# The scan's norms summed in four groups of 32 columns and spread by DMA, and output blocks fetched and split in pairs k, k+4

## The chip, the cores and the metric

The kernel runs on one NeuronCore of a Trainium2 chip. TensorE (PE) multiplies, VectorE (DVE) and ScalarE (ACT) do elementwise work, GpSimd (POOL) does a little, and SyncE (SP) issues nearly all DMAs, in order, from one queue. The metric is the device time of one execution in microseconds; lower is better.

## The reference

One layer of a hybrid encoder over 2048 tokens of width 1024: RMSNorm, an input projection, two mixers (a gated short convolution and a Mamba-2 scan), an output projection over both mixers' 2 x 1024 outputs, then a squared-ReLU MLP and a final RMSNorm. The part that the change touches is the grouped norm after the scan, and how its result enters the output projection:

```python
gated = (y * jax.nn.silu(z)).reshape(b, t, SSD_GROUPS, SSD_INNER // SSD_GROUPS)
gated = rmsnorm(gated, norm_w.reshape(SSD_GROUPS, SSD_INNER // SSD_GROUPS))
...
y = jnp.concatenate([y_a, y_b], axis=-1)
x = x + jnp.einsum("btc,cd->btd", y, w_out)
```

There are two groups of 512 channels. For every token and group one number is needed: the reciprocal root of the mean of 512 squares.

## The kernel before

Channels lie on partitions, tokens on the free axis. Tokens come in four blocks of 512 (TB); a block has four chunks of 128 (L). Every product in fp32 is made of three fp32r matmuls, high by high, low by high and high by low (`mm3`, L118 to L120, or L315 to L317 in `chain`), so every operand is split first: a cast on ACT gives the high part, a subtraction on DVE the low part. A tile framework decides the instruction order of each engine when the program is built; the order is then fixed.

The stages around the change, in order of time in the profile:

- `second_half` (about 440 to 950 us): the second half of the input projection, with scan chunks 0 to 15 (blocks 0 and 1) run beside it. At its end the scan's buffers are given back and the loads `rb<-ym_d` (L379) of the output projection's first operands take their place; the loads `wraw<-w_out` (L98) and `xt<-x` (L1643) follow in the same SP queue.
- `Output.pair` (to about 1040 us): the products of mixer A for blocks 0 and 1, a seven-product scheme.
- `Output.unit` 16 to 63 (to about 1350 us): units of 24 matmuls into a tile `pm`, first mixer A for blocks 2 and 3, then mixer B. Scan chunks 16 to 31 (blocks 2 and 3) run beside them. Units 48 to 63 take blocks 2 and 3 of mixer B; unit 50 is the first of block 3.

A norm is made at the last chunk of each block and group (`Scan.back`), eight times. `ssq` [128 x 512] holds the sums of squares over four channel tiles. It is split into `ahi` and `alo` (L180, L181), two matmuls with a matrix of ones sum over partitions and at the same time copy the sum to all 128 partitions (`pss`, L186, L187), then come root (L188, ACT) and reciprocal (L189, DVE), both on 128 x 512. For blocks 0 and 1 the result is stored (`rn_d<-ssq`, L1499) and loaded back as `rn` when it is needed (L1519); for blocks 2 and 3 it stays in SBUF.

`Output.fetch` loads two neighbouring channel tiles (`ry`, L1607), k and k+1. `Output.fill` scales each with its norm (mixer B, L1619), casts it (L1623) and subtracts (L1624), each [128 x 512], into `uh` and `ul`; a tile pair k and k+4 shares one `uh` buffer. Tiles 0 to 3 belong to group 0, tiles 4 to 7 to group 1. A unit multiplies k = 0 to 7 in that order.

Of the kernel before, what the change touches and what calls it, by code (L numbers as in the profile page):

```python
# [11 lines left out]
F32 = mybir.dt.float32  # L12
F32R = mybir.dt.float32r
AF = mybir.ActivationFunctionType
ALU = mybir.AluOpType

P = 128
# [23 lines left out]
def trunk(ctx: ExitStack, tc: tile.TileContext, x, w_in, w_dt, w_out, w_up, w_down, cvec, hrow, out):  # L41
# [19 lines left out]
    ym_d = [dram.tile([P, 7, TB], F32, name=f"ym_d{k}") for k in range(4)]  # L61
    wide = lambda n, k: [dram.tile([P, k, TH], F32, name=f"{n}_d{h}") for h in range(2)]
    xs_d, sz_d, ys_d, yn_d = wide("xs", 12), wide("sz", 8), wide("ys", 8), wide("yn", 8)
    rn_d = dram.tile([P, NBB, G, TB], F32, name="rn_d")
    dt_d = [dram.tile([P, 4, NC * 16], F32, name=f"dt_d{b}") for b in range(NB)]
    rd_d = [dram.tile([2, NC * 16, P], F32, name=f"rd_d{b}") for b in range(NB)]
    pd_d = dram.tile([P, TB], F32, name="pd_d")
# [20 lines left out]
    def col(base, i):  # L88
        return cv[:, base + i : base + i + 1]
# [1253 lines left out]
    class Scan:  # L1343
# [104 lines left out]
        def back(self, n):  # L1448

            b, g, c, h, ts, r0 = self.place(n)  # L1450
            t = self.got.pop(n)
            cT = t["bc"][:, 1]
            byhead = lambda a: a.rearrange("p (h d) -> p h d", h=HG)
            state = self.state[g]
            st = psum("tp", "st", 2)
            mm3(st, *t["btok"], *t["parts"], 0, 1)
            yo = psum("k4", "yo")
            for j in range(4):
                nc.tensor.matmul(yo[:, j * L : (j + 1) * L], state[:, j * P : (j + 1) * P], cT, start=True, stop=True)  # L1459
            yd = t["yd"]  # L1460
            for i in range(HG):
                nc.tensor.matmul(  # L1462
                    yd[(i % 2) * 64 : (i % 2) * 64 + 64, (i // 2) * L : (i // 2 + 1) * L],
                    byhead(t["xdt"])[:, i, :],
                    t["dec"][:, i % 2 * 4 + i // 2, :],
                    start=False,
                    stop=True,
                    skip_group_check=True,
                )
            y = t["y"]  # L1470
            t1 = self.tmp()
            nc.vector.tensor_tensor(out=byhead(state), in0=byhead(state), in1=t["cdec"], op=ALU.mult)
            nc.vector.tensor_tensor(out=state, in0=state, in1=st, op=ALU.add)
            nc.vector.tensor_tensor(out=t1, in0=yo, in1=t["eb"].rearrange("p j l -> p (j l)"), op=ALU.mult)
            nc.vector.tensor_tensor(out=t1, in0=t1, in1=yd, op=ALU.add)
            yield
            t3 = t1.rearrange("p (j l) -> p j l", j=4)
            nc.vector.tensor_tensor(out=y, in0=t3, in1=y, op=ALU.mult)
            yield
            nc.sync.dma_start(yn_d[h][:, 4 * g : 4 * g + 4, ts], y)  # L1480
            q4 = self.tmp().rearrange("p (j l) -> p j l", j=4)
            self.act = nc.scalar.activation(q4, y, AF.Square)
            nc.vector.tensor_tensor(out=q4[:, 0:2], in0=q4[:, 0:2], in1=q4[:, 2:4], op=ALU.add)
            if c == 0:
                self.ssq = self.sum_tile(b, g)
            ssq = self.ssq
            nc.vector.tensor_tensor(out=ssq[:, c * L : (c + 1) * L], in0=q4[:, 0], in1=q4[:, 1], op=ALU.add)
            if c == NC - 1:
                st = Rstd(None, self.part_tile, 512, TB)
                st.parts(ssq)  # L1490
            yield
            if c == NC - 1:
                if (b, g) == (NBB, 0):
                    ssq = uh.tile([P, TB], F32, tag="uh3", name="ssq", bufs=4)
                st.whole(ssq, "mw" if h else "tp")
                if h:
                    self.rn[b, g] = ssq
                else:
                    nc.sync.dma_start(rn_d[:, b, g], ssq)  # L1499
            yield  # L1500
            yield

# [4 lines left out]
                return self.tile([TB], "ssq", 1)  # L1507
            return uh.tile([P, TB], F32, tag="uh3", name="ssq", bufs=4)

        def part_tile(self, name):  # L1510
            if self.bufs == 1:
                return proj.e(name, TB)
            return uh.tile([P, TB], F32, tag="ul3", name=name, bufs=4)

        def norm(self, b, g):

            if (b, g) not in self.rn:
                t = self.rn[b, g] = uh.tile([P, TB], F32, tag="ul3", name="rn", bufs=4)
                nc.sync.dma_start(t, rn_d[:, b, g])  # L1519
            return self.rn[b, g]  # L1520

        def run(self, begin, end):
# [65 lines left out]
    class Output:  # L1588
# [14 lines left out]
        def fetch(self, i, b, k, raw):  # L1603

            t = raw("ry")
            src = (ys_d, yn_d)[i][b // NBB]
            nc.sync.dma_start(t, src[:, k : k + 2, b % NBB * TB : (b % NBB + 1) * TB])  # L1607
            return t

        def fill(self, i, b, c, k, t):  # L1610

            blk = self.y.setdefault((i, b), {})
            for n in range(2):
                f = k + n
                if f < 4:
                    self.places[f][c] = proj.place(c)
                hi, lo = (a[:, f // 4] for a in self.places[f % 4][c])
                if i:
                    nc.vector.scalar_tensor_tensor(  # L1619
                        out=t[:, n], in0=t[:, n], scalar=col(C_NSSD, f), in1=scan.norm(b, f // 4), op0=ALU.mult, op1=ALU.mult  # L1620
                    )
                with tc.issue_after(scan.act.ins) if (i, b) in ((1, 0), (1, 2)) else nullcontext():
                    nc.scalar.copy(hi, t[:, n])  # L1623
                nc.vector.tensor_tensor(out=lo, in0=t[:, n], in1=hi.bitcast(F32), op=ALU.subtract)  # L1624
                blk[f] = (hi, lo)

        def open(self, stack, ws):
            self.xp = stack.enter_context(tc.tile_pool(name="xp", bufs=1, reuse_waits="tile"))
# [69 lines left out]
        def unit(self, n, hook):  # L1698

            i, b, d = self.UNITS[n]  # L1700
            self.residual(n + 1)
            m = (2 * i + b // 2) * KD + d
            if b % 2 == 0:
                self.weights(m + 2)
            pm = psum("mm", "pm")
            whi, wlo = self.ws[m]
            for k in range(KD):
                if k == KD // 2:
                    hook(2 * n)
                mm3(pm, whi[:, k, :], wlo[:, k, :], *self.y[i, b][k], k, KD)  # L1710
            t = self.xt.pop(n)
            nc.vector.tensor_tensor(out=t, in0=pm, in1=t, op=ALU.add)
            nc.sync.dma_start(x1_d[b][:, d], t)
            if i and b < NBB:
                self.square(b, d, t)
            hook(2 * n + 1)
# [11 lines left out]
        def schedule(self):  # L1728
# [3 lines left out]

            def put(i, b, c, load, splits):
                def fetch():
                    held[i, b] = [self.fetch(i, b, k, self.raw) for k in range(0, KD, 2)]
                    if i and b < NBB:
                        for g in range(G):
                            scan.norm(b, g)

                self.todo.setdefault(load, []).append(fetch)  # L1740
                for j, at in enumerate(splits):
                    self.todo.setdefault(at, []).append(lambda j=j: self.fill(i, b, c, 2 * j, held[i, b][j]))

            put(0, 3, 0, 20, (22, 23, 23, 24))
            put(0, 2, 2, 25, (26, 27, 32, 32))
# [141 lines left out]
```

## Time and profile before

| what | us |
|---|---|
| median of 3 runs | 2596.71 (2595.24 to 2597.68) |
| profiled execution | 2599.74 |
| its span | 2598.0 |
| PE busy, of the span | 2572.3 |
| DVE busy | 1937.1 |
| ACT busy | 1407.0 |

The profiled execution is 1.74 us longer than its span and 3.03 us above the median of the runs. In a timeline, a row shows the start in us, the duration in us, engine, line, operation, output and input tiles, shapes, and in brackets how long the engine was idle before it and what ended the idle time. Matmuls overlap, so the distance of two starts is what a matmul costs, not its duration. In a view by stretches each engine's busy time in the stretch is given, then the granted PE clock, the busy share of the DMA engines and GB/s.

### The profile page before, as it was taken

To read this page: it belongs to the slowest core of one execution; us is meant where nothing else is said; L and a number is where in the kernel's file an instruction comes from. 1 tells how busy PE (TensorE), PEld (TensorE's weight loads), DVE (VectorE), ACT (ScalarE), POOL (GpSimd) and SP (SyncE) were. 2 spreads that over 40 slices of the span, in tenths; PEclk is the share of its full clock that TensorE was granted. 3 is DMA by queue.
4 is the path that set the end of the run, shared out by engine and by line. 5 is a ranking of instruction groups with operands and counts; after the bars stand their busy time and mean duration, and the time that the engine had idled before them with its cause. 6 is when DMAs were issued, how large, how long until landed. Compare 5 with 4: busy or idle time off the path is not lost.

```text
span 2598.0 us, 33641 instructions
## 1 busy us (share of the span) xinstructions
PE 2572.3 (99%) x12027; PEld 2120.2 (82%) x12027; DVE 1937.1 (75%) x2627; ACT 1407.0 (54%) x2147; POOL 79.2 (3%) x99
## 2 busy tenths in 40 slices
PE   9999999999999999999999999999999999999998
PEld 7788878788888878888888888888887888888887
DVE  8877777867778688889877765644448887888885
ACT  6554345876567566656336555755556444444433
POOL 2110010000000000000000000000000000000001
PEclk9999999999999999999999999999999999999999
DMA  4555665755555478997656885855557655665762
GB/s 175 175 191 188 218 238 184 238 171 174 178 168 176 158 251 281 291 294 243 201 186 231 300 313 219 291 196 212 183 201 252 187 175 154 219 207 179 238 203 78
DMA packets 256345, 546.40 MB, mean 210 GB/s; under 512 B 26673, under 2 KB 93873, under 8 KB 256177
## 3 DMA queue, kind: packets, MB, share of 16 engines
q1 hardware_dynamic: 255600, 543.34, 62.4%
q8 instruction: 94, 1.54, 0.2%
q10 hardware_dynamic: 576, 0.92, 0.1%
q14 instruction: 75, 0.61, 0.1%
HBM read 359.87 MB, written 184.29 MB: 209 GB/s over the span
## 4 chain that ended last, share of the span: by engine, by line
PE 88%; DVE 5%; DMA 3%; issue 2%; ACT 2%; POOL 0%; SPq 0%; POOLq 0%; DVEq 0%; ACTq 0%
PE px L315 14%; PE px L317 14%; PE px L316 14%; PE py L315 7%; PE py L316 7%; PE py L317 7%; PE pm L118 4%; PE pm L119 4%; PE pm L120 4%; PE pw L315 3%; PE pw L317 3%; PE pw L316 3%; PE yd L1462 1%; DVE ul L391 1%; PE yo L1459 1%
## 5 line engine op out<-in xcount | busy, mean ns | idle before, releaser
L315 PE MATMUL px<-uh,whi 128*128 128x512 f32 x1736 | 679.6, 392 | 7.7 <-DVE acc L1176 3.3
L317 PE MATMUL px<-uh,wlo 128*128 128x512 f32 x1736 | 676.2, 390 | 0.5 <-DVE wlo L104 0.5
L316 PE MATMUL px<-ul,whi 128*128 128x512 f32 x1736 | 675.8, 389 | 0.0
L315 PEld LDWEIGHTS px<-uh,whi 128*128 128x128 f32 x1736 | 325.9, 188 | 82.2 <-DVE acc L1176 4.1
L317 PEld LDWEIGHTS px<-uh,wlo 128*128 128x128 f32 x1736 | 325.9, 188 | 70.9 <-issue 1.8
L316 PEld LDWEIGHTS px<-ul,whi 128*128 128x128 f32 x1736 | 326.0, 188 | 66.3
L104 DVE TENSOR_TENSOR wlo<-wraw,whi 128x512 fp32r<-128x512 f32 (+1 forms) x213 | 219.0, 1029 | 197.4 <-ACT whi L103 196.4
L103 ACT CAST whi<-s 128x1024 fp32r<-128x1024 f32 x218 | 228.3, 1047 | 216.6 <-PE py L316 97.7
L315 PE MATMUL py<-uh,whi 128*128 128x512 f32 x868 | 339.2, 391 | 2.3 <-ACT eb L850 1.5
L103 ACT CAST whi<-wraw 128x1024 fp32r<-128x1024 f32 x214 | 192.2, 899 | 274.5 <-PE px L316 214.1
L317 PE MATMUL py<-uh,wlo 128*128 128x512 f32 x868 | 338.0, 389 | 0.0
L316 PE MATMUL py<-ul,whi 128*128 128x512 f32 x868 | 338.0, 389 | 0.0
L104 DVE TENSOR_TENSOR wlo<-s,whi 128x1024 fp32r<-128x1024 f32 x218 | 265.1, 1216 | 76.2 <-ACT whi L103 75.2
L118 PE MATMUL pm<-uh,whi 128*128 128x512 f32 (+1 forms) x520 | 200.1, 385 | 0.8 <-ACT z L601 0.7
L119 PE MATMUL pm<-ul,whi 128*128 128x512 f32 (+1 forms) x520 | 197.8, 381 | 0.5 <-DVE ul L231 0.5
L120 PE MATMUL pm<-uh,wlo 128*128 128x512 f32 (+1 forms) x520 | 197.5, 380 | 0.0
L315 PEld LDWEIGHTS py<-uh,whi 128*128 128x128 f32 x868 | 163.0, 188 | 38.6 <-ACT eb L850 1.9
L316 PEld LDWEIGHTS py<-ul,whi 128*128 128x128 f32 x868 | 163.0, 188 | 34.2 <-issue 0.8
L317 PEld LDWEIGHTS py<-uh,wlo 128*128 128x128 f32 x868 | 163.0, 188 | 33.8
L315 PE MATMUL pw<-uh,whi 128*128 128x512 f32 x434 | 169.3, 390 | 0.0
L316 PE MATMUL pw<-ul,whi 128*128 128x512 f32 x434 | 168.9, 389 | 0.0
L317 PE MATMUL pw<-uh,wlo 128*128 128x512 f32 x434 | 168.9, 389 | 0.0
(265 smaller groups left out, 3613.1 us busy)
## 6 DMA issues: line engine op xcount, KB each, us to landing
hid_d<-e SPq DMA_DIRECT2D x96, 512.0 KB, 3.6
rh<-hid_d SPq DMA_DIRECT2D x96, 512.0 KB, 4.3
wraw<-w_in SPq DMA_DIRECT2D x68, 512.0 KB, 4.0
wraw<-w_down SPq DMA_DIRECT2D x104, 256.0 KB, 3.6
wraw<-w_up SPq DMA_DIRECT2D x48, 512.0 KB, 4.6
dec<-rd_d SPq DMA_DIRECT2D x32, 512.0 KB, 5.4
wraw<-w_out SPq DMA_DIRECT2D x32, 512.0 KB, 5.6
sums_d<-s SPq DMA_DIRECT2D x32, 512.0 KB, 4.4
```

What stands on the lines that cost most here:

```text
L103: nc.scalar.copy(hi, raw)
L104: split["last"] = eng.tensor_tensor(out=lo, in0=raw, in1=hi.bitcast(F32), op=ALU.subtract)
L118: nc.tensor.matmul(out, whi, hi, start=(k == 0), stop=False)
L119: nc.tensor.matmul(out, whi, lo, start=False, stop=False)
L120: nc.tensor.matmul(out, wlo, hi, start=False, stop=(k == nk - 1))
L315: nc.tensor.matmul(p, hi, h[0], start=not seeded and k == 0, stop=False, **kw)
L316: nc.tensor.matmul(p, hi, h[1], start=False, stop=False, **kw)
L317: nc.tensor.matmul(p, lo, h[0], start=False, stop=(k == len(g) - 1), **kw)
L391: nc.vector.tensor_tensor(out=p[i][1], in0=t, in1=p[i][0].bitcast(F32), op=ALU.subtract)
L1459: nc.tensor.matmul(yo[:, j * L : (j + 1) * L], state[:, j * P : (j + 1) * P], cT, start=True, stop=True)
L1462: nc.tensor.matmul(yd[(i % 2) * 64 : (i % 2) * 64 + 64, (i // 2) * L : (i // 2 + 1) * L], byhead(t["xdt"])[:, i, :], t["dec"][:, i % 2 * 4 ...
```

## The change

The sums over partitions are made by four fp32 matmuls (`pn`), each with 32 columns of ones as weights and one chunk's 128 columns of `ssq` as moving data, into 32 partitions each of one PSUM tile. So `ssq` isn't split. Root and reciprocal work on 128 x 128. The result (128 x 128, of which rows 0, 32, 64 and 96 hold the four chunks) is stored for every norm; a second DMA reads these four rows and spreads them over 128 partitions as [128 x 512]. For blocks 0 and 1 this load stands where `rn` was loaded before; for blocks 2 and 3 it follows the store.

`fetch` loads tiles k and k+4 in one piece. `fill` scales both with their two norms, and makes one cast and one subtraction of [128 x 1024]. A unit multiplies in the order 0, 4, 1, 5, 2, 6, 3, 7.

```diff
@@ Scan.back
             nc.vector.tensor_tensor(out=ssq[:, c * L : (c + 1) * L], in0=q4[:, 0], in1=q4[:, 1], op=ALU.add)
+            yield
             if c == NC - 1:
-                st = Rstd(None, self.part_tile, 512, TB)
-                st.parts(ssq)
-            yield
-            if c == NC - 1:
-                if (b, g) == (NBB, 0):
-                    ssq = uh.tile([P, TB], F32, tag="uh3", name="ssq", bufs=4)
-                st.whole(ssq, "mw" if h else "tp")
+                pn = psum("mw", "pn") if h else psum("tp", "pn", 2)
+                for i in range(NC):
+                    nc.tensor.matmul(
+                        pn[i * 32 : i * 32 + 32, 0:L], ones[:, 0:32], ssq[:, i * L : (i + 1) * L], start=True, stop=True
+                    )
+                r = ssq[:, 0:L]
+                nc.scalar.activation(r, pn[:, 0:L], AF.Sqrt, bias=eps, scale=1.0 / 512)
+                nc.vector.reciprocal(out=r, in_=r)
+                nc.sync.dma_start(rn_d[b][g], r)
                 if h:
-                    self.rn[b, g] = ssq
-                else:
-                    nc.sync.dma_start(rn_d[:, b, g], ssq)
+                    self.rn[b, g] = self.norm_tile(b, g, "uh3" if (b, g) == (NBB, 0) else None)
@@ Scan
+        def norm_tile(self, b, g, tag):
+            t = uh.tile([P, TB], F32, tag=tag, name="rn", bufs=4) if tag else self.ssq
+            row = rn_d[b][g].rearrange("(q p) l -> p q l", p=32)[0]
+            nc.sync.dma_start(t.rearrange("p (q l) -> p q l", q=NC), row.partition_broadcast(P))
+            return t
@@ Output.fetch
-            nc.sync.dma_start(t, src[:, k : k + 2, b % NBB * TB : (b % NBB + 1) * TB])
+            nc.sync.dma_start(t, src[:, k : k + 5 : 4, b % NBB * TB : (b % NBB + 1) * TB])
@@ Output.fill
+            hi, lo = self.places[k][c] = proj.place(c)
+            if i:
+                for n in range(2):
+                    nc.vector.scalar_tensor_tensor(
+                        out=t[:, n], in0=t[:, n], scalar=col(C_NSSD, k + 4 * n), in1=scan.norm(b, n), op0=ALU.mult, op1=ALU.mult
+                    )
+            with tc.issue_after(scan.act.ins) if (i, b) in ((1, 0), (1, 2)) else nullcontext():
+                nc.scalar.copy(hi, t)
+            nc.vector.tensor_tensor(out=lo, in0=t, in1=hi.bitcast(F32), op=ALU.subtract)
             for n in range(2):
...
+                blk[k + 4 * n] = hi[:, n], lo[:, n]
@@ Output.unit
-            for k in range(KD):
+            for j in range(KD):
...
+                k = j // 2 + j % 2 * 4
+                mm3(pm, whi[:, k, :], wlo[:, k, :], *self.y[i, b][k], j, KD)
```

The built order of the instructions moves with it. Three places, each as it stands before and with the change.

The first is the end of `second_half`: the last norm of block 1 on DVE, from its sum of squares (L1487) on. `wlo` are weight splits, `s` weight sums, `eb` and `ea` evictions of the projection. Before:

```order
L1487 TENSOR_TENSOR ssq<-stmp 128x128
L181 TENSOR_TENSOR alo<-ssq,ahi 128x512
L269 TENSOR_TENSOR s_7941<-wraw 128x512
L234 TENSOR_TENSOR s_7941<-s_7941,wraw 128x512
L807 TENSOR_TENSOR eb<-px,s_7908 128x512
L234 TENSOR_TENSOR s_7985<-wraw 128x512
L189 RECIPROCAL ssq<-ssq 128x512
L104 TENSOR_TENSOR wlo<-s_7941,whi 128x1024
```

With the change:

```order
L1487 TENSOR_TENSOR ssq<-stmp 128x128
L104 TENSOR_TENSOR wlo<-wraw,whi 128x1024
L269 TENSOR_TENSOR s_7940<-wraw 128x512
L1497 RECIPROCAL ssq<-ssq 128x128
L234 TENSOR_TENSOR s_7940<-s_7940,wraw 128x512
L807 TENSOR_TENSOR eb<-px,s_7907 128x512
L234 TENSOR_TENSOR s_7984<-wraw 128x512
L104 TENSOR_TENSOR wlo<-s_7940,whi 128x1024
```

The split of `ssq` is gone, and the reciprocal stands before two weight sums and one eviction that it stood behind. On SP the store of this norm stays right behind `yn_d<-y`, with the loads `rb<-ym_d` behind it.

The second is DVE at the last norm, that of block 3 and group 1, and the operands of unit 50 (`ry` into `ul`). `xt<-pm` are evictions of units. Before, from the reciprocal on:

```order
L189 RECIPROCAL ssq<-ssq 128x512
L1712 TENSOR_TENSOR xt<-pm,xt 128x512
L104 TENSOR_TENSOR wlo<-wraw,whi 128x1024
L1726 TENSOR_TENSOR facc<-sq,facc 128x512
L1619 SCALAR_TENSOR_TENSOR ry<-ry,cv,ssq 128x512
L1712 TENSOR_TENSOR xt<-pm,xt 128x512
L1619 SCALAR_TENSOR_TENSOR ry<-ry,cv,ssq 128x512
L1624 TENSOR_TENSOR ul_11350<-ry,uh_11349 128x512
L181 TENSOR_TENSOR alo<-facc,ahi 128x512
L1624 TENSOR_TENSOR ul_11355<-ry,uh_11354 128x512
```

With the change, from the first scale that needs this norm:

```order
L1618 SCALAR_TENSOR_TENSOR ry<-ry,cv,ssq 128x512
L1713 TENSOR_TENSOR xt<-pm,xt 128x512
L1618 SCALAR_TENSOR_TENSOR ry<-ry,cv,ssq 128x512
L1623 TENSOR_TENSOR ul_11309<-ry,uh_11308 128x1024
L1618 SCALAR_TENSOR_TENSOR ry<-ry,cv,ssq 128x512
L1623 TENSOR_TENSOR ul_11329<-ry,uh_11328 128x1024
L189 RECIPROCAL facc<-facc 128x512
L1623 TENSOR_TENSOR ul_11361<-ry,uh_11360 128x1024
L1713 TENSOR_TENSOR xt<-pm,xt 128x512
L1618 SCALAR_TENSOR_TENSOR ry<-ry,cv,ssq 128x512
L189 RECIPROCAL facc<-facc 128x512
L1623 TENSOR_TENSOR ul_11385<-ry,uh_11384 128x1024
```

Before, four halves of group 0 were split further up, and only the four of group 1 waited for this norm; now all four pieces do, and two reciprocals of the next stage (`facc`) stand between them.

The third is PE at the same norm: a `pm` matmul of unit 47 is ahead of it and behind it in both. Before:

```order
L118 MATMUL pm<-uh_10208,whi 128x512
L186 MATMUL pss<-ahi,ones_r 128x512
L187 MATMUL pss<-alo,ones_r 128x512
L119 MATMUL pm<-ul_10209,whi 128x512
L120 MATMUL pm<-uh_10208,wlo 128x512
```

With the change:

```order
L118 MATMUL pm<-uh_10189,whi 128x512
L1492 MATMUL pn<-ssq,ones_r 32x128 x4
L119 MATMUL pm<-ul_10190,whi 128x512
L120 MATMUL pm<-uh_10189,wlo 128x512
```

Two matmuls of 512 columns become four of 128 columns. In two of the eight norms `pn` follows the scan's own fp32 matmuls `yd` directly; in one of these the fourth `pn` stands 41 rows further on.

More of the change, by code (lines that the diff above doesn't have):

```diff
@@ L63, in trunk @@
     xs_d, sz_d, ys_d, yn_d = wide("xs", 12), wide("sz", 8), wide("ys", 8), wide("yn", 8)
-    rn_d = dram.tile([P, NBB, G, TB], F32, name="rn_d")
+    rn_d = [[dram.tile([P, L], F32, name=f"rn_d{b}_{g}") for g in range(G)] for b in range(NB)]
     dt_d = [dram.tile([P, 4, NC * 16], F32, name=f"dt_d{b}") for b in range(NB)]
@@ L1508, in sum_tile @@
             return uh.tile([P, TB], F32, tag="uh3", name="ssq", bufs=4)
[L1510 to L1513, printed above, removed]
+        def norm_tile(self, b, g, tag):
[3 more added lines that the diff above has]
+            return t
         def norm(self, b, g):
             if (b, g) not in self.rn:
-                t = self.rn[b, g] = uh.tile([P, TB], F32, tag="ul3", name="rn", bufs=4)
-                nc.sync.dma_start(t, rn_d[:, b, g])
+                self.rn[b, g] = self.norm_tile(b, g, "ul3")
             return self.rn[b, g]
@@ L1612, in fill @@
             blk = self.y.setdefault((i, b), {})
-            for n in range(2):
[L1614 to L1625, printed above, removed]
+            hi, lo = self.places[k][c] = proj.place(c)
[7 more added lines that the diff above has]
+            nc.vector.tensor_tensor(out=lo, in0=t, in1=hi.bitcast(F32), op=ALU.subtract)
+            for n in range(2):
+                blk[k + 4 * n] = hi[:, n], lo[:, n]
         def open(self, stack, ws):
@@ L1706, in unit @@
             whi, wlo = self.ws[m]
-            for k in range(KD):
-                if k == KD // 2:
+            for j in range(KD):
+                if j == KD // 2:
                     hook(2 * n)
-                mm3(pm, whi[:, k, :], wlo[:, k, :], *self.y[i, b][k], k, KD)
+                k = j // 2 + j % 2 * 4
+                mm3(pm, whi[:, k, :], wlo[:, k, :], *self.y[i, b][k], j, KD)
             t = self.xt.pop(n)
@@ L1734, in fetch @@
                 def fetch():
-                    held[i, b] = [self.fetch(i, b, k, self.raw) for k in range(0, KD, 2)]
+                    held[i, b] = [self.fetch(i, b, k, self.raw) for k in range(4)]
                     if i and b < NBB:
@@ L1741, in put @@
                 for j, at in enumerate(splits):
-                    self.todo.setdefault(at, []).append(lambda j=j: self.fill(i, b, c, 2 * j, held[i, b][j]))
+                    self.todo.setdefault(at, []).append(lambda j=j: self.fill(i, b, c, j, held[i, b][j]))
             put(0, 3, 0, 20, (22, 23, 23, 24))
```

## The prediction

> **What bounds the kernel now.** I read the page's first part, then the waits and idle times of PE by stretch, then what PE waited for in the stretch that the change touches.
>
> ```profile
> span 2598.0 us, 33641 instructions
> PE 2572.3 (99%) x12027; PEld 2120.2 (82%) x12027; DVE 1937.1 (75%) x2627; ACT 1407.0 (54%) x2147; POOL 79.2 (3%) x99
> ```
>
> PE is busy for 2572.3 of 2598.0 us. Only two things can move the time by much: the PE work itself, and PE's idle time, 25.8 us in all. A shorter DVE or ACT is worth nothing unless PE waits for it. The timeline of PE shows these waits between the first norm (its PE work is at about 580 us) and the end of the units, apart from two of 0.24 and 0.15 us that I leave as they are:
>
> ```profile
> 959.90 0.50 PE L315 MATMUL px<-uh,whi 128*128 128x512 f32 x1 [0.56 <-DVE xt L1669]
> 963.96 0.47 PE L315 MATMUL px<-uh,whi 128*128 128x512 f32 x1 [1.01 <-DVE xt L1669]
> 968.08 0.50 PE L317 MATMUL px<-uh,wlo 128*128 128x512 f32 x1 [0.52 <-DVE wlo L104]
> 971.02 0.50 PE L315 MATMUL py<-uh,whi 128*128 128x512 f32 x1 [0.39 <-DVE s L234]
> 1071.95 0.49 PE L118 MATMUL st<-xtok,btok 128*128 128x512 f32 x1 [1.20 <-ACT xtok L1438]
> ```
>
> The bracket at the end of a row is the wait: 0.56 + 1.01 + 0.52 + 0.39 = 2.48 us at 959 to 971, and 1.20 us at 1072. That is all that can be won from waits here, 3.68 us.
>
> **Where the 2.48 us come from.** The last norm of block 1 stands in front of the loads of the next stage. The SP queue (timeline of SP) issues one store at 914.77, then nothing until the norm's store at 925.86:
>
> ```profile
> 914.77 0.37 SPq L1480 DMA_DIRECT2D yn_d<-y  x1
> 925.86 0.32 SPq L1499 DMA_DIRECT2D rn_d<-ssq  x1
> ```
>
> DVE shows why; the store waits for this reciprocal, which ends at 925.83:
>
> ```profile
> 922.48 3.35 DVE L189 RECIPROCAL ssq<-ssq 128x512 f32<-128x512 f32 x1
> ```
>
> The view by stretches shows what this does to the DMA engines (the column before the last is their share, then GB/s):
>
> ```profile
> 920.00:925.00 5.00, 5.00 (x24) 4.13 (x23) 4.36 (x4) 3.85 (x5) 0.00 (x0) 1.00 0.00 0
> 930.00:940.00 10.00, 10.00 (x46) 8.25 (x45) 6.99 (x8) 6.71 (x9) 0.00 (x0) 1.00 1.00 361
> ```
>
> They stand still while SP is held, then run at 1.00. Forty us later, operands of PE are still late; of the casts on ACT one waits 4.31 us for a weight load:
>
> ```profile
> 965.71 1.05 ACT L103 CAST whi<-wraw 128x1024 fp32r<-128x1024 f32 x1 [4.31 <-DMA wraw<-w_out]
> ```
>
> **The change, part by part.** *Reciprocals.* The profile's groups by line give the prices:
>
> ```profile
> L189 DVE RECIPROCAL ssq<-ssq 128x512 f32<-128x512 f32 x8 | 26.8, 3350 | 4.7 <-ACT ssq L188 4.7
> L1624 DVE TENSOR_TENSOR ul<-ry,uh 128x512 fp32r<-128x512 f32 x48 | 31.7, 685 | 4.7 <-ACT uh L1623 4.7
> L391 DVE TENSOR_TENSOR ul<-first,uh 128x1024 fp32r<-128x1024 f32 x4 | 4.7, 1219 | 2.4 <-ACT uh L390 2.4
> ```
>
> A reciprocal of 512 columns takes 3350 ns, so 128 columns take about 3350/4 = 840 ns. Eight of them free 8 x 2.5 = 20 us of DVE. The eight splits (a cast on ACT, a subtraction on DVE) go too. All of this lies beside PE's work and counts for nothing by itself, but it moves the store above. In the new order the reciprocal is the second instruction after the weight split that follows the sum. Before, it began at 922.48 and took 3.35. It now ends at about 920.6: the new order takes out the split of `ssq`, two weight sums and an eviction ahead of it. The store goes out 5 us sooner, and the DMA engines use 5 us in which they stood still. That is more than each of the four waits (1.01 at most) and than their sum. I take the whole 2.48 us. Bounds: nothing (if the loads are held by something else), and 2.48.
>
> *The wait at 1072.* It is for an ACT cast, which waits for DVE, which did this just before:
>
> ```profile
> 1060.25 2.74 DVE L1619 SCALAR_TENSOR_TENSOR ry<-ry,cv,rn 128x512 f32<-128x512 f32 x4 [1.90 <-DMA rn<-rn_d]
> 1062.90 3.35 DVE L189 RECIPROCAL ssq<-ssq 128x512 f32<-128x512 f32 x1
> ```
>
> DVE waits 1.90 us for the norm load and then has four scales and a 3.35 us reciprocal ahead of the scan's work. In the new order one scale and a short reciprocal stand there. That is over 4 us less ahead of an operand that is 1.20 us late. I take 1.20; bounds 0 and 1.20.
>
> *PE's work.* Two fp32r matmuls of a norm start 0.22 apart and the next follows as fast, so a norm costs 2 x 0.227 = 0.454:
>
> ```profile
> 1127.31 0.39 PE L186 MATMUL pss<-ahi,ones_r 128*128 128x512 f32 x1
> 1127.53 0.39 PE L187 MATMUL pss<-alo,ones_r 128*128 128x512 f32 x1
> ```
>
> An fp32 matmul leaves two records. For `pn` with 32 weight columns and 128 moving columns there is no row. The nearest: `pd` (32 weight columns, 512 moving), `yo` (128 weight columns, 128 moving) and `yd` (64 weight columns, 128 moving).
>
> ```profile
> 257.81 0.39 PE L317 MATMUL py<-uh,wlo 128*128 128x512 f32 x1
> 258.13 1.07 PE L667 MATMUL pd<-nb,rdt 128*32 128x512 f32 x8
> 259.13 0.50 PE L315 MATMUL py<-uh,whi 128*128 128x512 f32 x1
> 259.46 0.39 PE L316 MATMUL py<-ul,whi 128*128 128x512 f32 x1
> 1140.15 1.05 PE L1459 MATMUL yo<-bc,state 128*128 128x128 f32 x8
> 1141.13 1.09 PE L1462 MATMUL yd<-dec,stmp 128*64 128x128 f32 x16
> ```
>
> Eight records of `pd` take 1.00 us (258.13 to 259.13), though each moves four times `pn`'s columns. Eight of `yo` take 0.98, sixteen of `yd` 1.02: half the weight columns, half the time per record, 64 ns, since two halves of the array work at once. So eight records of `pn` take at most 0.99 and, at half of `yd`'s price per record, 0.26. Entering and leaving fp32 costs 0.09 and 0.10 (257.81 to 258.13 and 259.13 to 259.46 against 0.227), nothing to enter directly behind `yd`. A norm thus costs between 0.26 and 1.18, against 0.454: over eight norms -1.6 to +5.8. I take 45 ns per record, 0.36, nearer to the low end because `pd` with four times the columns stays at 1.00; with edges (shared in some) 0.52, so 8 x 0.06 = +0.5.
>
> *Wider splits.* Two subtractions of 685 become one of 1219, so 24 x 0.15 = 3.6 us less on DVE, and about as much on ACT. PE's work covers both; nothing.
>
> *DMAs.* Eight stores of 64 KB replace four of 256; four loads of 256 KB are added, and all eight loads go in pieces of 512 B. `xd<-xs_d` has the load's shape, `yn_d<-y` the pieces of the store:
>
> ```profile
> L1499 SPq DMA_DIRECT2D rn_d<-ssq x4: 319/323/332, 588.1 to 925.9; - x4
> DMA to landing us min/median/max: 2.4/2.4/2.6
> L1384 SPq DMA_DIRECT2D xd<-xs_d x32: 370/377/507, 468.3 to 1200.2; - x32
> DMA to landing us min/median/max: 2.7/4.6/6.8
> L1480 SPq DMA_DIRECT2D yn_d<-y x32: 370/380/1102, 489.9 to 1248.9; - x32
> DMA to landing us min/median/max: 2.3/4.1/8.5
> L1519 SPq DMA_DIRECT2D rn<-rn_d x4: 382/424/565, 1052.4 to 1131.7; - x4
> DMA to landing us min/median/max: 5.7/7.2/8.0
> ```
>
> Each row of a DMA is followed by its tile's time from issue to landing (minimum, median, maximum). In blocks 2 and 3 SP must wait for the store to land before it issues the load, 2.4 us by the store of before. Behind it wait residual loads (`xt`, one unit ahead, 24 x 0.227 = 5.4 us) and chunk loads, a chunk ahead. The lead covers it; without cover it would be 4 x 2.4 = 9.6 us.
>
> *Unit 50.* Here the cover is thin. Before:
>
> ```profile
> 1263.03 3.35 DVE L189 RECIPROCAL ssq<-ssq 128x512 f32<-128x512 f32 x1 [1.52 <-ACT ssq L188]
> 1279.35 0.68 DVE L1624 TENSOR_TENSOR ul<-ry,uh 128x512 fp32r<-128x512 f32 x1
> 1274.63 0.39 PE L118 MATMUL pm<-uh,whi 128*128 128x512 f32 x1
> 1278.26 0.39 PE L119 MATMUL pm<-ul,whi 128*128 128x512 f32 x1
> 1280.30 0.62 PE L119 MATMUL pm<-ul,whi 128*128 128x512 f32 x2
> ```
>
> The norm was ready at 1266.4, the last operand of unit 50 at 1280.0, and PE took it as the second matmul of the row at 1280.30, at about 1280.6: 0.6 us to spare. Now the reciprocal ends at about 1263.3, the store lands 2.4 later (bounds 2.3 and 8.5), the load another 4.6 later (bounds 2.7 and 8.0), so the norm comes at 1270.3. From there the DVE order gives: scale, eviction, scale, split, scale, split, reciprocal, split; at 0.66, 0.60, 0.66, 1.15, 0.66, 1.15, 3.26 and 1.22 us that is 9.4 us to the third piece's low part. PE reaches it 16 matmuls into unit 50, at 1278.26. It is late by 1270.3 + 9.4 - 1278.3 = 1.4 us. Each us by which the norm is later costs one; at 1268.9 it costs nothing. I take 1.4.
>
> The Trainium skill's "DMA: Bandwidth & Descriptors", section "Anatomy of one DMA", says that a DMA costs about 2.0 us whatever its size, mostly the receipt of the write, plus bytes by 436 GB/s. That speaks against the change, since a quarter of the bytes doesn't make the store a quarter as long. The 2.4 us of the 256 KB store agree (2.6 by the rule). By it, as an estimate, store and load take 2.15 + 2.6 = 4.75 us, unit 50 waits for nothing and the sum is 1.4 us lower.
>
> **Sum.** -2.48 - 1.20 + 0.5 + 1.4 = -1.8 us. The profiled execution took 2599.74, so 2597.9; the median of the runs lies 3.03 below it, so the forecast is 2594.9. A measurement of this kernel can tell about 0.2% from no change, 5.2 us, so this is no difference.
>
> **Rivals.**
>
> 1. *The freed DMA time wins nothing.* For it: the DMA engines are still full at 930 to 940, so they may have no time to give, and SP also waits for evictions that PE sets. Against it: 5 us of still engines. The waits stay: +0.5 + 1.4 = +1.9, 2598.6.
> 2. *`pn` costs the full array's price.* The four groups share their rows, and if nothing overlaps each record takes `yo`'s 124 ns. Against it: `yd` overlaps two halves. Then -3.68 + 5.8 + 1.4 = +3.5, 2600.2. The Trainium skill's "TensorE: Matmul & The Clock Gate", section "The mechanism", says that weight loads overlap running matmuls only in other row groups; by that rule this is the case. The trace speaks against it with `yd`'s 64 ns.
> 3. *The norm comes too late for unit 50.* If store and load take the longest of their rows, 8.5 and 8.0, the norm comes at 1279.8, and DVE, whose next instruction waits for it, holds up evictions and scan: 10.9 us late, -3.68 + 0.5 + 10.9 = +7.7, 2604.4, slower. It decides from a norm at about 1277.3 on. Against it: both were the longest of 32 or 64.
> 4. *More than the waits goes.* With all waits gone, `pn` at 0.26 without edges and no wait at unit 50: -3.68 - 1.6 = -5.3, 2591.4, just under the bound.
>
> **How the numbers follow.** Forecast 0.58, rival 1 0.17, rival 2 0.07, rival 3 0.10, rival 4 0.08. Slower by over 0.2% is rival 3 and a part of an unknown wait in the new order, 0.13. Faster is rival 4 and the low end of the forecast, 0.13. The rest, 0.74, is within 0.2%. The range reaches from rival 4 to a norm at about 1275: 2591.4 to 2602.
>
> **What would show it.** The store of block 1's last norm at about 921, not 925.86, and no DMA share of 0.00 at 920; no waits at 959 to 971 and at 1072; four `pn` with eight records in 0.3 to 0.5 us; a wait of PE at unit 50, about 1278, between 0 and 4 us, with DVE waiting for the load before its first scale. It would be wrong if `pn` took a us, if new waits came in `Output.pair`, whose order changed too, or if SP held back weights behind the stores.

## The result, and the profile after

The changed kernel takes 2630.93 us (median of 4 runs, 2628.86 to 2633.96) against 2597.19 us of the kernel before (2595.24 to 2601.29): 1.0129 times as long, 95% interval 1.0111 to 1.0146. That is 33.7 us slower; the forecast was 2594.9, with a range to 2602. The profiled execution took 2631.94 us. The first part of its page:

```profile
span 2629.9 us, 33699 instructions
PE 2585.4 (98%) x12075; PEld 2126.3 (81%) x12075; DVE 1913.4 (73%) x2595; ACT 1399.5 (53%) x2115; POOL 75.7 (3%) x99
```

The span is 31.9 us longer. PE is busy 13.1 us longer (2585.4 against 2572.3) and idle 18.8 us longer (44.5 against 25.7), although it has only 48 records more in 12,075. So there are two things to find: new waits, and matmuls that take longer.

**What was won.** The timeline of SP around the last norm of block 1:

```profile
921.12 0.32 SPq L1498 DMA_DIRECT2D rn_d<-ssq  x1
921.49 1.86 SPq L379 DMA_DIRECT2D rb<-ym_d  x4
```

The store goes out at 921.12 (925.86 before), and the loads `rb<-ym_d` follow at once. The view by stretches has no still DMA engines any more (share 0.52, 157 GB/s; before 0.00):

```profile
920.00:925.00 5.00, 5.00 (x24) 4.14 (x23) 3.80 (x6) 3.49 (x5) 0.00 (x0) 1.00 0.52 157
```

Of the waits of PE at 959 to 971, 2.48 us before, one is left, a single row of PE's timeline:

```profile
969.89 0.47 PE L315 MATMUL py<-uh,whi 128*128 128x512 f32 x1 [0.33 <-DVE xt L1669]
```

**What was lost.** PE's waits from 1001 to 1320 (who, for whom: us in total, times, longest); the kernel before has one row there, the 1.2 us at 1072:

```profile
PE st L118 <- ACT xtok L1438: 12.3, 3, 7.7
PE ptb L1419 <- DVE state L1473: 3.7, 1, 3.7
PE st L119 <- DVE stmp L1440: 3.0, 3, 1.4
PE pm L118 <- ACT uh L1622: 2.8, 1, 2.8
...
```

From 1.2 us to 25.1, three smaller rows included. The longest is in the timeline of PE:

```profile
1074.10 0.80 PE L118 MATMUL st<-xtok,btok 128*128 128x512 f32 x1 [7.67 <-ACT xtok L1438]
```

It is where the wait of 1.20 us at 1072 stood, which the forecast had going away. PE waits for a cast on ACT. ACT's timeline shows what stands ahead of that cast, a cast of weights that waits 7.46 us for its load:

```profile
1069.63 1.04 ACT L103 CAST whi<-wraw 128x1024 fp32r<-128x1024 f32 x1 [7.46 <-DMA wraw<-w_out]
```

SP shows when that load was issued, and what stands around it:

```profile
1047.94 1.10 SPq L1515 DMA_DIRECT2D rn<-rn_d  x2
...
1053.54 1.30 SPq L98 DMA_DIRECT2D wraw<-w_out  x1
...
1060.99 0.33 SPq L1498 DMA_DIRECT2D rn_d<-ssq  x1
...
1070.49 0.38 SPq L1515 DMA_DIRECT2D rn<-rn_d  x1
```

The weights were issued at 1053.54 (within a row that spans 1.30 us) and landed at 1069.6, 16 us later. Ahead of them in the queue are the two loads of block 0's norms (1047.94). These are late themselves; on DVE the two scales that need them wait 3.69 and 3.49 us:

```profile
1059.35 0.75 DVE L1618 SCALAR_TENSOR_TENSOR ry<-ry,cv,rn 128x512 f32<-128x512 f32 x1 [3.69 <-DMA rn<-rn_d]
...
1064.99 0.75 DVE L1618 SCALAR_TENSOR_TENSOR ry<-ry,cv,rn 128x512 f32<-128x512 f32 x1 [3.49 <-DMA rn<-rn_d]
```

They landed at about 1059 and 1065, some 11 and 16 us after their issue. The answer for the tile `rn` holds all five loads of that name:

```profile
L1515 SPq DMA_DIRECT2D rn<-rn_d x5: 377/506/602, 1047.9 to 1146.8; - x5
...
DMA to landing us min/median/max: 9.3/10.8/16.4
```

Before, the four loads took 5.7, 7.2 and 8.0 us (minimum, median, maximum). And while they run, nearly nothing else does. The view by stretches at 1054 to 1062, before and with the change (the last two columns are the share of the 16 DMA engines and GB/s):

```profile
1054.00:1062.00 8.00, 8.00 (x54) 6.64 (x53) 5.58 (x10) 6.17 (x12) 0.00 (x0) 1.00 1.06 391
```

```profile
1054.00:1062.00 8.00, 8.00 (x49) 6.47 (x46) 3.81 (x6) 3.07 (x8) 0.00 (x0) 1.00 0.37 62
```

391 GB/s before, 62 now, and 780 of the 832 packets of this stretch are smaller than 2 KB (644 of 1972 before). A load of 256 KB that goes on 128 partitions in 512 pieces holds up everything that SP issued behind it: the weights, the norm's own store (1060.99; the load that waits for it goes out at 1070.49), the chunk's operands behind that.

**The longer matmuls.** The view by stretches again; the column after POOL is the granted clock of PE:

```profile
1068.60:1082.20 13.60, 6.73 (x30) 5.30 (x31) 8.59 (x11) 3.66 (x4) 0.00 (x0) 0.50 0.61 147
1095.90:1099.30 3.40, 1.66 (x7) 0.84 (x6) 3.27 (x5) 3.01 (x10) 0.00 (x0) 1.00 1.00 304
1099.30:1102.70 3.40, 3.40 (x25) 2.85 (x24) 1.80 (x3) 2.54 (x3) 0.00 (x0) 0.50 0.79 262
```

From 1068.6 on, while PE still waits for the cast, it is granted half the clock, for 13.6 us; 5.5 us of these are the rest of the wait. It is granted half for 3.4 us again at 1099. Two neighbouring matmuls of 512 columns start 0.43 us apart while that holds, against 0.227:

```profile
1308.65 0.63 PE L120 MATMUL pm<-uh,wlo 128*128 128x512 f32 x1
1309.08 0.63 PE L118 MATMUL pm<-uh,whi 128*128 128x512 f32 x1
```

The trace has five such stretches between 1068 and 1311, one at each group of waits, 30.7 us in all. PE's busy time in them is 22.3 us. By the distance of the matmuls, 0.43 against 0.227, a little under half of it, some 10.5 us by this estimate, is the price of the lower clock: most of the 13.1. What the rest is, no row shows. The Trainium skill's "TensorE: Matmul & The Clock Gate", "Part 1: The HAM clock gate", says that the clock falls to a half after an idle window of about 3.4 us, and that these windows run on whatever the kernel does. The lengths agree: 13.65, 3.41, 6.83, 3.41 and 3.41 us, and the five starts lie whole multiples of 3.41 us apart. But the window need not be idle as a whole: from 1095.9 to 1099.3, the stretch ahead of the second one, PE was busy for about half of the time by the row above. Nor does every wait bring the half clock: in padded_norms (below) PE waits 2.06 us at 1070 and 2.36 us at 1282, and the granted clock from 1060 to 1290 is 1.00. How busy is busy enough, the runs don't show.

### The profile page after: what moved, and what is told of

It reads as the page before. It is cut to its first block, busy times and chain, and to the rows that moved or that the text cites. A ratio compares the mean times of both kernels' runs of the same rounds, so it can differ in the third digit from the quotient of the medians.

```text
span 2629.9 us, 33699 instructions
## 1 busy us (share of the span) xinstructions
PE 2585.4 (98%) x12075; PEld 2126.3 (81%) x12075; DVE 1913.4 (73%) x2595; ACT 1399.5 (53%) x2115; POOL 75.7 (3%) x99
## 4 chain that ended last, share of the span: by engine, by line
PE 61%; issue 24%; DMA 7%; DVE 4%; ACT 2%; SPq 0%; POOL 0%; POOLq 0%; DVEq 0%; ACTq 0%
PE px L315 10%; PE px L317 10%; PE px L316 10%; PE py L315 5%; PE py L316 5%; PE py L317 5%; PE pw L315 2%; PE pw L317 2%; PE pw L316 2%; PE pm L119 2%; PE pm L120 2%; PE pm L118 2%; DMA rn<-rn_d 1%; DMA x_d<-xt 1%; PE yd L1462 1%
```

## The experiments

The theory after the first look: the price is the *source* of the norm's load. All 128 partitions read the same four rows of 512 B, 16 KB apart in DRAM, and these 512 reads are served one after the other ("hot rows"). The rivals: pieces of 512 B are slow whatever they read ("small pieces"); SP is held by the store that the load has to wait for ("round trip"); y's pieces now need both norms at once ("pairs").

### spread_rows: each partition reads its own rows

The store writes 128 rows of which 32 at a time are equal, so a partition can take its values from rows of its own.

```diff
-            row = rn_d[b][g].rearrange("(q p) l -> p q l", p=32)[0]
-            nc.sync.dma_start(t.rearrange("p (q l) -> p q l", q=NC), row.partition_broadcast(P))
+            rows = rn_d[b][g].rearrange("(q s) l -> s q l", s=32)
+            for r in range(4):
+                nc.sync.dma_start(t[32 * r : 32 * r + 32].rearrange("p (q l) -> p q l", q=NC), rows)
```

> The norm is stored as in the change (64 KB, 128 rows of 512 B), but its load goes in four quarters of 32 partitions, each partition reading its own four of the 128 equal rows instead of the same four for all: the same 512 pieces of 512 B, the same store ahead, three more issues on SP per load. Theory 'hot rows' (512 reads of four rows are served one after the other at about 45 GB/s and hold up all DMAs behind): the loads move at 200 GB/s or more, PE's 18.8 us of new waits and the half clock behind them go, time 2593 to 2601. Theory 'small pieces' (512 B pieces are the price): unchanged, 2627 to 2635. Theory 'round trip' (SP held by the store that the load waits for): unchanged, 2620 to 2635. Theory 'pairs' (the fetch and split of blocks k and k+4): unchanged, 2627 to 2635.

Measured: 2597.02 us, 0.9994 of the kernel before (0.9984 to 1.0004). All of the 33.7 us are gone. The page, the tile `rn` (four DMAs to a load now), the same stretch of the DMA engines, and PE's waits from 1001 to 1320:

```profile
span 2590.4 us, 33725 instructions
PE 2571.9 (99%) x12075; PEld 2118.8 (82%) x12075; DVE 1913.4 (74%) x2595; ACT 1400.8 (54%) x2115; POOL 78.4 (3%) x99
```

```profile
L1516 SPq DMA_DIRECT2D rn<-rn_d x20: 303/420/677, 1045.5 to 1140.3; - x20
...
DMA to landing us min/median/max: 1.8/5.5/8.3
```

```profile
1054.00:1062.00 8.00, 8.00 (x41) 6.67 (x40) 7.77 (x13) 4.21 (x8) 0.00 (x0) 1.00 0.87 261
```

```profile
PE pn L1492 <- DVE facc L1728: 1.3, 1, 1.3
```

The stretch moves 261 GB/s, the wait at 1072 is gone altogether, and what is left is 1.3 us of another kind, at the last norm's `pn` (point 7 below). "Small pieces", "round trip" and "pairs" fall: piece size, store, order and pairs are those of the change.

### compact_row: one row of 2 KB for all

```diff
-    rn_d = ... dram.tile([P, L], F32, name=f"rn_d{b}_{g}")
+    rn_d = ... dram.tile([NC, L], F32, name=f"rn_d{b}_{g}")
-                nc.sync.dma_start(rn_d[b][g], r)
+                nc.sync.dma_start(rn_d[b][g], r[0:P:32])
...
+            nc.sync.dma_start(t, rn_d[b][g].rearrange("q l -> (q l)").partition_broadcast(P))
```

> Only one partition of each group of 32 is stored (4 rows of 512 B, side by side: 2 KB), and the load sends these 2 KB to every partition: 128 pieces of 2 KB, 256 KB as before. 'Hot rows', if the number of reads of a spot counts: 128 reads take 1.5 us, time 2593 to 2600; if the bytes read from a spot count, still 5 us per load, 2622 to 2632. 'Small pieces': 2593 to 2600 too. 'Round trip': 2620 to 2635. 'Pairs': 2627 to 2635.

Measured: 2598.05 us, 1.0000 (0.9991 to 1.0009). The same bytes go to all partitions from one place, and it is not slow. By itself this leaves open whether the number of reads (128 in place of 512) or the layout did it.

### norms_alone: the change without the pairs

The functions `fetch`, `fill` and `unit` are those of the kernel before, the rest is the change.

> The change's norms with their store and load, while y is fetched and split in the order of the kernel before (blocks k and k+1, a split each; the unit's matmuls in order of k). 'Hot rows', 'small pieces' and 'round trip': the loads stay as slow, time 2620 to 2634 (less where a unit needs only the first norm for its first pieces). 'Pairs': 2593 to 2600.

Measured: 2629.94 us, 1.0126 (1.0111 to 1.0141). The whole loss is in the norms. PE's waits for the cast on ACT from 1001 to 1320 are those of the change: 12.8 us in 3 times, there 12.3 in 3.

### load_probe: the load by itself

A kernel of nothing but loads to 128 partitions, each followed by a tiny copy on DVE that waits for it:

```diff
+    for name, go in tests.items():
+        for _ in range(4):
+            t = sb.tile([P, 1024], F32, tag="t", name=name, bufs=1)
+            go(t)
+            nc.vector.tensor_copy(out=seen, in_=t[:, 0:1])
```

> Loads to 128 partitions alone on the DMA engines, each kind four times, each waited for before the next; nothing of the reference is computed. Kinds (tile names): plain 256 KB (own 2 KB rows), far16k (four rows of 512 B, 16 KB apart, to all partitions, as in the change), spread (four quarters, own rows), far17k, far18k, far4k, far1k (the four rows at these distances), same (one row of 512 B four times), flat2k and flat4k (2 KB and 4 KB side by side to all). 'Hot rows': plain 2.3 to 3 us, spread 3 to 4.5, far16k 7 to 8 (256 KB at 45 GB/s is 5.8 us, and about 2 us for any DMA), same at least as long. If reads of one row wait for one another whatever the distance, far17k, far18k and far4k take what far16k takes; if the 16 KB distance is what counts, they take 3 to 5. 'Small pieces': spread and all of the 512 B kinds take what far16k takes.

DVE's timeline, the second load of each kind; the bracket is the time from the copy before to the landing:

```profile
54.59 0.15 DVE L82 COPY seen<-far16k 128x1 f32<-128x1 f32 x1 [7.74 <-DMA far16k<-d]
77.14 0.15 DVE L82 COPY seen<-spread 128x1 f32<-128x1 f32 x1 [3.36 <-DMA spread<-d]
91.12 0.15 DVE L82 COPY seen<-far17k 128x1 f32<-128x1 f32 x1 [3.25 <-DMA far17k<-d]
138.74 0.15 DVE L82 COPY seen<-far1k 128x1 f32<-128x1 f32 x1 [3.23 <-DMA far1k<-d]
161.76 0.15 DVE L82 COPY seen<-same 128x1 f32<-128x1 f32 x1 [7.73 <-DMA same<-d]
185.15 0.15 DVE L82 COPY seen<-flat2k 128x1 f32<-128x1 f32 x1 [3.29 <-DMA flat2k<-d]
```

The change's load takes 7.74 us alone on the chip, and its rows moved to 17 KB distance 3.25, with the same number of reads of each row. Four rows 16 KB apart are as slow as one row for all 512 reads (7.73), four rows 1 or 17 KB apart as quick as 2 KB in one piece. So it is neither the small pieces nor the sharing alone, but shared rows at a distance at which they get in each other's way. Of the two outcomes put on record for far17k, far18k and far4k, the distance decides for the first two (3.25 and 3.23 us); at 4 KB the load is in between (4.81).

### padded_rows: one number in the change

```diff
-    rn_d = ... dram.tile([P, L], F32, name=f"rn_d{b}_{g}")
+    rn_d = ... dram.tile([P, L + 8], F32, name=f"rn_d{b}_{g}")[:, 0:L]
```

> The change with one number edited: the rows of the norm's DRAM tile lie 544 B apart instead of 512 B, so the four rows that a load reads are 17 KB apart instead of 16. Packets, their 512 bytes, the 128 reads of each row, the stores, the queue and the order are those of the change. 'Hot rows by their distance' (rows 16 KB apart are served by one place, as load_probe showed with 7.4 us against 3.1): the loads land in 3 to 5.5 us, no waits of PE over 2.1 us between 1050 and 1320, time 2593 to 2600. 'Each row read 128 times is the price, at whatever distance': 2620 to 2632.

Measured: 2600.89 us, 1.0005 (0.9996 to 1.0013). Eight unused columns of DRAM take the loss away. The loads:

```profile
L1515 SPq DMA_DIRECT2D rn<-rn_d x5: 377/505/632, 1049.3 to 1129.7; - x5
...
DMA to landing us min/median/max: 3.5/5.8/7.7
```

3.5, 5.8 and 7.7 us against 9.3, 10.8 and 16.4, with the same 512 pieces in one DMA. This is the narrowest test of the cause within the kernel, and it holds. Two figures lie a little above what was expected: the longest load (7.7 us, not 5.5) and the time (2600.89, not 2600; the kernel before took 2599.69 beside it). PE's longest wait between 1050 and 1320, 1.96 us, lies within the 2.1.

### pairs_alone: the other half of the change

The kernel before with `fetch`, `fill` and `unit` of the change.

> The kernel before with blocks k and k+4 fetched and split in one piece; the norms as before (512 columns, no load for blocks 2 and 3). 'Hot rows': this part is worth nothing, the waits of the kernel before at 959 to 971 and at 1072 stay, 2593 to 2601. 'Pairs' (already unlikely after norms_alone): over 2610. Should it be over 2603, both of a pair's pieces waiting for the second norm is a price of its own.

Measured: 2601.05 us, 1.0008 (0.9999 to 1.0017): no difference that can be told from none. The waits at 959 to 971 stay, 1.7 us together; at 1072, 0.37 us is left.

### hot_two_blocks: half of the loads healed

As padded_rows, with `L + 8 * (b >= NBB)`.

> As padded_rows, but the four loads of blocks 0 and 1 keep the rows 16 KB apart; those of blocks 2 and 3 get 17 KB. 'Hot rows': two such loads go one behind the other at 1048 (the norms of block 0), so DVE still waits some 7 us there for the second and PE 3 to 8 us at 1066, with half the clock behind it; at 1158 and 1294 no waits are left. Time 2602 to 2618. If the store, its receipt and the load behind it in blocks 2 and 3 were the price, 2625 or more would stay.

Measured: 2617.46 us, 1.0069 (1.0056 to 1.0082), about half of the loss (0.0069 of 0.0129). PE's two longest waits from 1001 to 1320:

```profile
PE st L118 <- ACT xtok L1438: 7.9, 1, 7.9
PE ptb L1419 <- DVE state L1473: 3.6, 1, 3.6
```

The wait at 1072 (7.9 us) belongs to the loads of block 0. The one at 1159 (3.6), which I had given to the loads of block 2, stayed: there too DVE waits for a load of `rn`, one of block 1's. At unit 50, where none was expected either, 2.0 us are left. In these points the expectation was wrong; the time was inside its range.

### distance_probe and rows_probe: which distances, and does sharing matter

> As load_probe, from one of the inputs, nothing of the reference computed. four1k to four32k: four rows of 512 B at that distance, each read by all 128 partitions. own1k to own17k: 512 different rows at that distance, each read once. 'One place for addresses 16 KB apart': four16k, four32k and own16k take 7 us or more, own17k and four17k 3.1. 'Reading the same row again is the price': own16k takes about 3 us, like own17k.

```profile
81.89 0.15 DVE L82 COPY seen<-four8k 128x1 f32<-128x1 f32 x1 [7.87 <-DMA four8k<-w_up]
234.45 0.15 DVE L82 COPY seen<-own16k 128x1 f32<-128x1 f32 x1 [3.15 <-DMA own16k<-w_up]
```

Four shared rows 8, 16 or 32 KB apart are all slow (7.87 in the row; 7.6 and 7.5 us median from issue to landing at 16 and 32 KB). But 512 different rows at 16 KB, each read once, take 3.15. So "one place for all addresses 16 KB apart" falls as I had put it. The second probe was to tell whether it is the repeated reading or a higher part of the address:

> As distance_probe. four64k to four2m: four rows at that distance, each read by all 128 partitions. eight, sixt, thirt: 8, 16 and 32 rows at 1 or 16 KB, read by 64, 32 and 16 partitions each, in 2, 4 and 8 DMAs (so up to 3 us more from issuing). If only the low part of the address chooses the place, all of four64k to four2m and all kinds at 16 KB take 7 us and more. If higher parts choose too, some of the far ones take 3 to 5, and the 16 KB kinds get shorter with the number of rows, as 512 rows at 16 KB took 3.1.

```profile
65.97 0.15 DVE L86 COPY seen<-four64k 128x1 f32<-128x1 f32 x1 [7.42 <-DMA four64k<-w_up]
107.51 0.15 DVE L86 COPY seen<-four256k 128x1 f32<-128x1 f32 x1 [3.55 <-DMA four256k<-w_up]
171.87 0.15 DVE L86 COPY seen<-eight1k 128x1 f32<-128x1 f32 x1 [3.80 <-DMA eight1k<-w_up]
197.00 0.15 DVE L86 COPY seen<-eight16k 128x1 f32<-128x1 f32 x1 [8.62 <-DMA eight16k<-w_up]
```

Four rows 64 KB apart are still slow (7.42), at 128 KB half-way (4.4 median to landing), at 256 KB quick. Eight rows, each read by 64 partitions, are as slow at 16 KB (8.62) as one row, and quick at 1 KB (3.80, two DMAs). Sixteen rows, each read by 32 partitions, still take 7.3 to 9.0 us at 16 KB against 3.4 to 3.5 at 1 KB; with 32 rows, each read by 16, little is left (6.2 to 6.8 against 5.2, eight DMAs each). So it isn't the repeated reading of one row alone. The runs would fit a place that many reads share and that rows up to about 64 KB apart have in common at multiples of 8 KB, while rows further apart find other places; this would also explain why 512 rows over 8 MB aren't slow. That explanation is argued, not shown, and four rows 2 MB apart (4.8 us median to landing) speak against its simplest form. What such a place is inside the memory, no run shows. The Trainium skill's "DMA: Bandwidth & Descriptors", section "Latency and other measured facts", has a row on copies whose rows lie at large powers of two (207 GB/s at a pitch of 512 KiB, 164 at 2 MiB, 103 at 4 MiB, and 214 again with 4 KiB of padding); it names aliasing of HBM channels as an inference that isn't verified. The runs agree in kind and not in size: with shared rows it hurts in full from a distance of 8 KB on (7.87 us), and 1 KB on top of 16 KB cures it (3.25).

### spread_norms and padded_norms: the best of both

As norms_alone, with the loads of spread_rows or of padded_rows.

> The change's norms with the loads of spread_rows, and y fetched and split as in the kernel before (as in norms_alone). pairs_alone measured +1.4 us over the kernel before and spread_rows -0.7; if both parts add up, the norms without the pairs come to -2 us or a little more, near the -1.8 of the forecast: 0.9980 to 0.9998 of the kernel before. If the pairs do no harm, it stays at spread_rows's 0.9994.

Measured: 2595.40 us, 0.9989 (0.9980 to 0.9998): 2.8 us by the ratio, the only version whose interval lies below 1. It beats the kernel before by about a thousandth, less than the 0.2% that I count as faster. The interval also holds spread_rows's 0.9994, so the times don't decide whether the pairs cost anything.

> As spread_norms, but with the loads of padded_rows (one DMA of 512 pieces, rows 17 KB apart). The loads of padded_rows landed at 3.5 to 7.7 us, those of spread_rows at 1.8 to 8.3 with four issues each: 0.9985 to 1.0010 of the kernel before; against norms_alone (1.0126) only the distance of the rows differs, so over 1.008 would speak against it.

Measured: 2598.72 us, 1.0001 (0.9992 to 1.0010). Against norms_alone, from which it differs by the rows' distance alone, all of the loss is gone again.

| version | time against the kernel before | PE's waits 900 to 1045, 1045 to 1330 (us) |
|---|---|---|
| kernel before | 1 | 2.6, 1.2 |
| the change | 1.0129 | 0.5, 24.9 |
| norms_alone | 1.0126 | 1.3, 25.9 |
| hot_two_blocks | 1.0069 | 1.5, 16.7 |
| compact_row | 1.0000 | 2.9, 2.7 |
| padded_rows | 1.0005 | 3.1, 4.7 |
| padded_norms | 1.0001 | 0.9, 4.7 |
| pairs_alone | 1.0008 | 2.9, 0.7 |
| spread_rows | 0.9994 | 0.5, 1.3 |
| spread_norms | 0.9989 | 0.7, 0.8 |

The last column adds up the brackets of PE's timeline, from one profiled execution each; spread_norms, padded_norms and norms_alone are without the pairs. The two versions whose loads go in quarters from own rows have the fewest waits.

## Why the prediction was wrong, point by point

1. **The step that failed is the price of the added loads** ("*DMAs.*"). I took it from `xd<-xs_d`, which "has the load's shape", at 4.6 us with a lower bound of 2.7; the upper one, 8.0, is from the old loads of `rn`. `xd` has the shape, but its 512 pieces come from 512 different addresses; the norm's come from four. The term was mis-sized at its source: 7.4 us alone against 3.1 for the same load at another distance (load_probe), and in the kernel 9.3 to 16.4 for the five loads named `rn` and 6.6 to 9.8 for the three named `ssq`. Nearest rows were chosen by size and count of the pieces; what address each piece reads was not looked at, though the diff says it (`[0]` of 32 rows, `partition_broadcast`). Sharing alone would not have been enough to find it: the kernel before already sends eight rows to all partitions (L1386), but these lie side by side, and its view of DMAs shows no such price (count, size, median us to landing):

```profile
dec<-rd_d SPq DMA_DIRECT2D x32, 512.0 KB, 5.4
```

2. **"The lead covers it" failed with it.** I asked whether the norm itself comes in time, and priced its lateness without cover at 9.6 us. The dearer part was what stands *behind* the load: 62 GB/s for 8 us, weights 16 us under way, and PE's 7.67 us for a cast that has nothing to do with the norm. None of the rivals named this. The prediction's last sentence came nearest, with SP holding back weights "behind the stores" as a sign of being wrong, but it gave that no price and no chance, and it was the loads that held them back.
3. **Rival 3, the slower one, had the sign and not the place.** It put the late load at unit 50, at 10.9 us. There the store went out at 1291.43, the load at 1294.12, and DVE's scale got it at 1303.91:

```profile
1291.43 0.32 SPq L1498 DMA_DIRECT2D rn_d<-ssq  x1
...
1294.12 0.40 SPq L1515 DMA_DIRECT2D ssq<-rn_d  x1
```

```profile
1290.46 0.95 DVE L1497 RECIPROCAL ssq<-ssq 128x128 f32<-128x128 f32 x1
...
1303.91 0.75 DVE L1618 SCALAR_TENSOR_TENSOR ry<-ry,cv,ssq 128x512 f32<-128x512 f32 x1 [8.16 <-DMA ssq<-rn_d]
```

   That is 9.8 us for a load whose longest I had put at 8.0, and PE's waits behind it add up to 4.5 us (2.81, 0.81 and 0.83 between 1305 and 1314) plus some 1.6 of half clock (the last of the five stretches). Some three quarters of the new waits (19.0 us) are at 1066 to 1182, where the norms of blocks 0 to 2 are loaded. In the healed versions unit 50 shows nothing of the load in spread_rows, 2.0 us in compact_row and padded_rows: the 1.4 that I took lies between.
4. **The half clock was in no term.** Some 10.5 us, a third of the longer span, are matmuls at a lower clock behind the waits. I priced each wait at its own length; behind the two waits at 1097 (0.61 and 1.13) the clock cost nearly as much again (some 1.6 us).
5. **The 2.48 us: the mechanism was right, the size only in part.** The store at 921.12 (I had "about 921"), no still DMA engines, and 0.33 us of waits left at 970. But other executions with the same order up to there still show 0.5 to 3.1 us of waits between 900 and 1045 (last table), so "the whole 2.48" was the best case. In compact_row a part of the wait moved to the chunk's loads (1.9 us at 977 to 979).
6. **The wait at 1072** is gone in spread_rows and compact_row; padded_rows has 0.95 us and padded_norms 2.06 us there, for another operand of the same matmuls. Right where the loads are quick, and not sure.
7. **`pn` was right.** Eight records take 0.35 us (582.83 to 583.18; forecast 0.36), and the norm costs 1.01 - 2 x 0.227 = 0.56 us with its edges (forecast 0.52). Rival 2 (full-array price) falls, and PE's busy time in spread_rows is 2571.9 against 2572.3:

```profile
582.51 0.39 PE L317 MATMUL py<-uh,wlo 128*128 128x512 f32 x1
582.83 0.43 PE L1492 MATMUL pn<-ssq,ones_r 128*32 128x128 f32 x8
583.18 0.50 PE L315 MATMUL px<-uh,whi 128*128 128x512 f32 x1
583.52 0.39 PE L316 MATMUL px<-ul,whi 128*128 128x512 f32 x1
```

   The rule of the Trainium skill that rival 2 went by (weight loads overlap only in other row groups; "TensorE: Matmul & The Clock Gate", "The mechanism") would have given 1 us here; the trace does not bear that out for four column groups, 44 ns a record.

   "*Wider splits*", which the prediction put at nothing, came with a wait that no term had: at the last norm PE stands still until a DVE instruction of the next stage (`facc`) is done. The row of the changed kernel:

```profile
1287.81 0.43 PE L1492 MATMUL pn<-ssq,ones_r 128*32 128x128 f32 x8 [1.45 <-DVE facc L1727]
```

   It is 1.45 us here, 1.29 in spread_rows, 1.26 in hot_two_blocks, 1.12 in padded_rows and 0.66 in compact_row, and pairs_alone has 0.34 before its `pss`. The versions without the pairs (norms_alone, spread_norms, padded_norms, the kernel before) have none there. So it goes with the pairs; why PE has to wait for that instruction, no run shows.
8. **The sum.** With the load healed in three ways, the whole change measures 0.9994, 1.0000 and 1.0005 of the kernel before. The forecast of -1.8 us (0.9993) lies inside the intervals of the first two and 0.0003 below that of padded_rows. The rest of the reasoning is thus not refuted; that each of its terms is right is not shown. Where the total comes out near, that is in part luck, since the wait at the last `pn` and the waits left at 900 to 1045 weren't in it. One sum is wrong as it stands: a norm at about 1275 gives, by the prediction's own terms, -3.68 + 0.5 + 6.1 = +2.9 us or 2599.6, not the range's end of 2602, which belongs to a norm at about 1277.4. The measured time lies far outside either.

## What to carry to other kernels

When a load is new, compare it with a row of the trace that has the same *source pattern*, not only the same pieces: how many partitions read a row, and how far apart these rows lie (8, 16, 32 and 64 KB were slow). Four rows read by all partitions took 7.7 us alone at 16 KB distance and 3.3 at 17 KB; in the kernel the DMA engines moved 62 GB/s while two such loads ran, 391 before, and the weights queued behind them took 16 us. A layout of [128, 128] fp32 (512 B a row) puts every 16th row at such a step, 8 KB; padding by eight columns, packing the rows side by side, or giving each reader its own copy each took the price away. And a wait of some us on the matrix engine should be priced with the half clock that can come with it (some 10.5 us here beside 25.1 us of waits).

## What was not expected of the hardware

512 reads of 512 B from four shared rows take about 4.5 us more when the rows lie 16 KB apart (7.74) than when they lie 17 KB apart (3.25), some 9 ns a read. Four rows 1, 2, 17 or 18 KB, 256 or 512 KB or 1 MB apart don't show it, four rows 8, 16, 32 or 64 KB apart do in full, 4 KB, 128 KB and 2 MB in part (4.4 to 4.8 us median to landing). And the granted clock fell to a half for 3.4 us after a window in which PE had been busy for half of the time.
